# A hybrid attention layer's late phase: another order of the last products, an earlier copy out of PSUM, and one set of loads moved to GpSimd

## The chip, the cores and the metric

The kernel runs as one program on one core of a Trainium2 chip. The metric is the device time of one execution in microseconds (us); smaller is better. Times named "span" run from the first to the last instruction that the profile shows.

## The reference, cut to what matters

```python
def reference(x, w_in, w_out, t5_bias, na_rpb, ln_gain, ln_bias):    # x: (1, 512, 2048), all fp32
    h = einsum('bsd,de->bse', x, w_in[0])                            # 2048 -> 8192 columns
    qa, ka, va, ga, qb, kb, vb, gb = split(h)                        # eight blocks of 1024 columns
    ya = dilated_attention(qa, ka, va, t5_bias)                      # group A: 16 heads of 64
    yb = neighbourhood_attention(qb, kb, vb, na_rpb)                 # group B: 16 heads of 64
    y = concatenate([merge(ya) * silu(ga), merge(yb) * silu(gb)])    # (512, 2048)
    out = einsum('bse,ed->bsd', y, w_out[0])                         # 2048 -> 2048
    return layer_norm(2 ** 0.25 * x + out, ln_gain, ln_bias)
```

## The kernel before

Products of fp32 numbers are made from three float32r matmuls each: every operand is split into a high part (a copy by ScalarE, tiles `wh`, `yk`, `th`) and a low part (a subtraction by VectorE, tiles `wl`, `tl`), and TensorE adds high x high, low x high and high x low. A weight tile of 128x1024 so costs one ScalarE copy and one VectorE subtraction before TensorE may read it.

The work has three stages. First the projections of q, k, v and a part of the gates, in seven products of half size (Strassen's scheme) per block. Then 128 steps of attention: heads go in pairs, 16 pairs of 8 steps each; in each step TensorE makes scores (`scores`), VectorE and ScalarE the softmax, TensorE transposes the probabilities of two steps earlier (`turn`), and every fourth step multiplies them with v (`values`). Between these, `fill` feeds TensorE matmuls of the remaining gates and of the output projection's first columns. Last comes the late phase: the rest of the output projection, the residual and the layer norm.

Names in the attention stage. `turn` transposes into a PSUM bank `pt`, of which there are two; ScalarE copies it to `th`, VectorE subtracts into `tl`, and then the bank is free. Once a pair, in its step 2, `share` transposes the reciprocals of the softmax sums (`den`) into a `pt` bank as well; ScalarE copies that bank to a small row (`tmp<-pt`, 8x128), GpSimd writes it to DRAM (`rc_d`) and later reads it back, spread over the partitions, as `rc`. In the kernel before, copy and write stand in `send`, which runs at the end of the step (`later(0, ...)`, `close`), behind what was put there earlier. `gated` divides an older pair's output by `rc` (VectorE), copies it to the high part `yk` (ScalarE) and writes it to `y_d` in DRAM (GpSimd).

Names in the late phase. The four column groups of the output (512 columns each, numbered 0 to 3) are tiles z[t][dc] for the row blocks t = 0 to 3. Groups 0 and 1 are made in Strassen's seven products (`product`, numbered 1 to 7), groups 2 and 3 directly; the second half of group 3 is "the last column group" (`third` for t = 0, 1, and a loop at the end for t = 2, 3). `jobs` is the list of TensorE work, about 2.7 us each, and `at(n, ...)` hangs work of the other engines on job n; `project` runs them in source order. `convert` splits a weight two jobs ahead, `fetch` loads it through SyncE. `again` reads a pair's y back from `y_d` into one of two buffers (`ysum`), `combine_y`, `high_y` and `low_y` make the sums that Strassen's products need; `starts` lists the jobs of the eight `combine_y`. Work of `put`, `onto`, `done` and `stats` adds the products into z and takes the statistics for the layer norm. `norm` is the layer norm of a row block: VectorE centres, ScalarE scales by 1/sigma, and the bias is added by an accumulating DMA from GpSimd (`z<-in_lbias`); then SyncE stores. `last_norm`, for t = 3, adds the bias on VectorE instead; its bias rows come from matmuls.

What sets the order: each engine takes its instructions in order, and each queue (SyncE's and GpSimd's DMA issues among them) as well. Within the loops the order is the source's (`manual_schedule` for all engines). Behind the loops, for t = 2 and 3, only VectorE is held to the source's order in the kernel before; the other engines' order was set by a scheduler.

Of the kernel before, what the change touches and what calls it, by code (L numbers as in the profile page):

```python
# [6 lines left out]
F32 = mybir.dt.float32  # L7
# [59 lines left out]
AWAKE = 9  # L67
# [4 lines left out]
def hybrid_layer(tc, xT, xn, w_in, w_early, w_mid, w_gate, w_out, t5x, brow, rpb, cmask, eye, gain, lbias, out):  # L72
    nc = tc.nc
    from contextlib import ExitStack
    with ExitStack() as ctx:
# [482 lines left out]
        def later(k, fn, dve=False):  # L558


            tasks.setdefault(step[0] + k, []).append((fn, dve))
# [192 lines left out]
        def share(i):  # L754

            turn8 = bank(pst, "pt")[0:8, 0:128]
            nc.tensor.transpose(turn8, dens[i], ident)

            def send():
                nc.scalar.activation(row, turn8, AF.Copy)  # L760
                nc.gpsimd.dma_start(rc_d[i], row)
                later(1, spread)

            def spread():
                while held and i > 0 and i - 1 not in divided:
                    behind_min(1)
                rc = rc_ring.next("rc")
                for a in range(2):
                    nc.gpsimd.dma_start(rc[64 * a:64 * a + 64], _view(rc_d, 1024 * i + 512 * a, [[0, 64], [1, 512]]))
                rcs[i] = rc  # L770

            later(0, send)
# [103 lines left out]
        late_tiles += [t_d[m][u] for m in (2, 0, 1) for u in range(4)]  # L876
        late_tiles += [w_out[m] for m in (*range(12, 16), *range(28, 32))] + [t_d[3][u] for u in range(4)]
# [95 lines left out]
        c01r, c23r = Ring("n8", "n9"), Ring("n10", "n11")  # L973
        c1_tags = ("n0", "n1", "n2", "n3", "n4", "n6", "n5", "n7")

        def again(i):
            cut_y[i] = yr.next("ysum")[:, :1024].rearrange("p (n q) -> p n q", n=4)
            nc.sync.dma_start(cut_y[i].rearrange("p n q -> p (n q)"), y_d[i].rearrange("p n q -> p (n q)"))
# [58 lines left out]
        def last_weight(u):  # L1037
            wts[u + 4] = [slot(f"r{2 * u + m}", F32R, "wlast") for m in range(2)]
            split(W[28 + u], *wts[u + 4])
# [12 lines left out]
        def norm(t):  # L1052
# [8 lines left out]
            def rescale(i):  # L1061
                zt = z[t][i]
                if t == 2 and i == 3:
                    nc.vector.scalar_tensor_tensor(zt, zt, rs, bb[0], op0=ALU.mult, op1=ALU.add)
                else:
                    nc.scalar.activation(zt, zt, AF.Copy, scale=rs)
                    nc.gpsimd.dma_start(zt, _view(lbias, 512 * i, [[0, 128], [1, 512]]), accum_op=ALU.add)
                nc.sync.dma_start(out[t * 128:t * 128 + 128, 512 * i:512 * i + 512], zt)
# [6 lines left out]
            for i in (0, 2, 3):  # L1075
                centre(i)
                rescale(i)

        accs3 = {}
# [35 lines left out]
        for t in range(4):  # L1115
            at((21, 22, 23, 25)[t], lambda t=t: done(2, t, o2[t]))
        at(34, lambda: done(3, 0, accs3[0]), lambda: norm(0))
        at(36, lambda: done(3, 1, accs3[1]), lambda: norm(1))
        for i in (2, 1):
            at(33 - i, lambda i=i: nc.vector.tensor_tensor(z[3][i], z[3][i], gb[i], ALU.mult))  # L1120
# [5 lines left out]
        with tc.manual_schedule(engines=engines):  # L1126
# [6 lines left out]
            for n in range(132):  # L1133
# [50 lines left out]
                if n in (129, 131):  # L1184
                    project((n - 133) // 2)
# [4 lines left out]
        def shift_rows():  # L1190

            raw, parts = slot("u0", F32, "lnraw"), slot("s0", F32R, "lnparts")
            for i, src in enumerate((gain, lbias)):
                nc.sync.dma_start(raw[:, 12 * i:12 * i + 12].rearrange("p (c j) -> p c j", c=3),
                                  _view(src, 0, [[4, 128], [512, 3], [1, 4]]))
            split(raw[:, :24], parts[:, :24], parts[:, 24:48])
            groups = slot("s1", F32R, "lnrows")
            groups = [groups[:, 512 * i:512 * i + 512] for i in range(3)]
            for r, at in enumerate((0, 24, 0, 12, 36)):
                for c in range(3):  # L1200
                    nc.sync.dma_start(f(groups[c][r:r + 1]), f(parts[:, at + 4 * c:at + 4 * c + 4]))
            return groups

        def last_norm(rows):
# [6 lines left out]
            nc.scalar.activation(rs, mv[:, 1:2], AF.Sqrt, bias=eps)  # L1211

# [4 lines left out]
            queues = [nc.sync, nc.scalar]  # L1217
# [29 lines left out]
        rows = shift_rows()  # L1247
        nms = small.tile([128, 8], F32R, name="nms", bufs=1)
        nc.gpsimd.memset(f(nms), 1.0)
        for t in (2, 3):  # L1250
            acc = bank(pacc, "acc")
            cuts = (slice(0, 256), slice(256, 512)) if t == 3 else (slice(0, 512),)
            accs = [acc] if len(cuts) == 1 else [acc, bank(pss, "sc")]
            for o, part in zip(accs, cuts):
                for u in range(4, 8):
                    list(out_mms(o, t, u, *wts[u], u == 4, u == 7, part))
            if t == 3:
                idle = bank(pss, "sc")
                for _ in range(AWAKE):
                    nc.tensor.matmul(idle, yk[8][:, 0, 0, 0:128], wts[4][0][:, 0:512], start=True, stop=True)  # L1260
            with tc.manual_schedule(engines={mybir.EngineType.DVE}):
                if t == 2:
                    home("t7", 0, 2, 3)
                    for m in range(2):
                        put(0, m + 2, p1[m])
                        stats(0, m + 2)
                    nc.vector.tensor_tensor(z[3][0], z[3][0], gb[0], ALU.mult)
                for m, part in enumerate(cuts):
                    finish(3, t, accs[m], part, 3 + m)
                if t < 3:  # L1270
                    norm(t)
                else:
                    last_norm(rows)
# [65 lines left out]
```

## Time and profile before

| | us |
|---|---|
| median of 3 runs (985.71 to 987.35) | 986.62 |
| the profiled execution | 986.07 |
| its span | 984.3 |
| TensorE busy | 959.6 |
| VectorE busy | 797.3 |
| ScalarE busy | 525.0 |
| GpSimd busy | 219.7 |

The attention stage lies at about 580 to 841 us of the span, the late phase behind it. The profile models the end of a matmul, and matmuls overlap by that model (one of 512 columns is shown as 0.39 us long while the next starts 0.23 us later); so a stall of TensorE is longer than the idle time shown, by the overlap that did not happen.

### The profile page before, as it was taken

What the parts mean: (1) busy time and instruction counts of PE and PEld (TensorE: products, weight loads), DVE (VectorE), ACT (ScalarE), POOL (GpSimd) and SP (SyncE); (2) the same over time, 40 slices, a digit from 0 to 9 for tenths busy, and PEclk for the clock granted to TensorE, in tenths of its full rate; (3) what the DMA queues carried; (4) which work ended last, traced back from release to release, by engine and by line L of the source; (5) the groups of instructions that cost most, each with busy time, mean ns of one, the idle gap of its engine ahead of it and who ended that gap; (6) DMA issues with size and microseconds to landing.
All of it is one profiled execution on the core that took longest, in us unless ns stands there. A gap on an engine that the chain in (4) does not pass through costs nothing.

```text
span 984.3 us, 14233 instructions
## 1 busy us (share of the span) xinstructions
PE 959.6 (97%) x4741; PEld 794.4 (81%) x4741; DVE 797.3 (81%) x1219; ACT 525.0 (53%) x900; POOL 219.7 (22%) x410
## 2 busy tenths in 40 slices
PE   9999999999999999999999999999999999999994
PEld 7878888888888889988888888887878777687883
DVE  8897787779689798897899757888778787789775
ACT  7454443444444444444454457777777777654531
POOL 1006656635741101111111001111111101100021
PEclk9999999999999999999999999999999999999997
DMA  9725796797595296744984887787877877676766
GB/s 339 268 83 124 251 308 205 197 287 212 146 375 189 106 346 202 257 160 147 318 259 143 273 265 252 233 261 241 276 240 269 301 244 233 214 252 226 261 115 175
DMA packets 131273, 227.75 MB, mean 231 GB/s; under 512 B 51247, under 2 KB 71599, under 8 KB 131200
## 3 DMA queue, kind: packets, MB, share of 16 engines
q1 hardware_dynamic: 110544, 179.39, 55.8%
q0 software_dynamic: 20080, 46.81, 16.1%
q8 instruction: 37, 0.61, 0.3%
q10 hardware_dynamic: 576, 0.66, 0.2%
q14 instruction: 36, 0.29, 0.1%
HBM read 169.66 MB, written 57.08 MB: 230 GB/s over the span
## 4 chain that ended last, share of the span: by engine, by line
PE 86%; DVE 5%; ACT 4%; DMA 2%; issue 2%; POOL 0%; DVEq 0%; SPq 0%; ACTq 0%; POOLq 0%
PE acc L405 16%; PE acc L407 16%; PE acc L406 15%; PE acc L601 8%; PE acc L811 5%; PE acc L928 4%; PE pt L726 4%; PE pv L748 4%; PE sc L707 2%; PE sc L706 2%; PE acc L281 2%; PE acc L282 2%; PE acc L283 1%; PE pt L262 1%; PE acc L398 1%
## 5 line engine op out<-in xcount | busy, mean ns | idle before, releaser
L378 ACT ACTIVATE wh<-braw 128x1024 fp32r<-128x1024 f32 x182 | 193.2, 1062 | 268.5 <-PE acc L406 201.0
L383 DVE TENSOR_TENSOR wl<-braw,wh 128x1024 fp32r<-128x1024 f32 x182 | 222.0, 1222 | 41.3 <-ACT wh L378 41.2
L405 PE MATMUL acc<-wh,xk 128*128 128x512 f32 x384 | 151.3, 394 | 0.0
L407 PE MATMUL acc<-wl,xk 128*128 128x512 f32 x384 | 149.7, 390 | 0.0
L406 PE MATMUL acc<-wh,xk 128*128 128x512 f32 x384 | 149.5, 389 | 0.0
L374 DVE TENSOR_TENSOR braw<-braw 128x1024 f32<-128x1024 f32 x104 | 128.4, 1235 | 0.1
L405 PE MATMUL acc<-wh,op 128*128 128x512 f32 x288 | 113.1, 393 | 0.0
L407 PE MATMUL acc<-wl,op 128*128 128x512 f32 x288 | 112.2, 390 | 0.0
L406 PE MATMUL acc<-wh,op 128*128 128x512 f32 x288 | 112.1, 389 | 0.0
L732 DVE TENSOR_TENSOR tl<-pt,th 128x256 fp32r<-128x256 f32 (+1 forms) x128 | 71.1, 556 | 31.6 <-ACT th L731 29.7
L407 PEld LDWEIGHTS acc<-wl,xk 128*128 128x128 f32 x384 | 72.1, 188 | 15.3
L405 PEld LDWEIGHTS acc<-wh,xk 128*128 128x128 f32 x384 | 72.1, 188 | 15.2 <-ACT bias L153 0.9
L406 PEld LDWEIGHTS acc<-wh,xk 128*128 128x128 f32 x384 | 72.2, 188 | 14.5
L601 PE MATMUL acc<-xk,wh 128*128 128x512 f32 x256 | 80.9, 407 | 0.0
L731 ACT ACTIVATE th<-pt 128x256 fp32r<-128x256 f32 (+1 forms) x128 | 62.4, 488 | 31.2 <-PE pt L726 29.3
L663 DVE CUSTOM_DVE_ANT_0 s<-sc,biases 128x512 f32<-128x512 f32 (+2 forms) x128 | 67.7, 529 | 9.6 <-PE sc L707 8.9
L667 ACT ACTIVATE p<-s,mn 128x512 f32<-128x512 f32 (+1 forms) x96 | 62.3, 649 | 24.5 <-DVE mn L663 24.0
L811 PE MATMUL acc<-wh,yk 128*128 128x512 f32 x192 | 67.7, 404 | 0.0
L163 POOL DMA_DIRECT2D bias<-rows_d x128 | 61.3, 487 | 15.2 <-DMA bias<-rows_d 6.2
L407 PEld LDWEIGHTS acc<-wl,op 128*128 128x128 f32 x288 | 54.1, 188 | 11.4
L406 PEld LDWEIGHTS acc<-wh,op 128*128 128x128 f32 x288 | 54.1, 188 | 11.0
L405 PEld LDWEIGHTS acc<-wh,op 128*128 128x128 f32 x288 | 54.1, 188 | 10.8
(202 smaller groups left out, 1864.5 us busy)
## 6 DMA issues: line engine op xcount, KB each, us to landing
braw<-in_w_in SPq DMA_DIRECT2D x96, 512.0 KB
k_d<-kst SPq DMA_DIRECT2D x64, 128.0 KB
q_d<-kst SPq DMA_DIRECT2D x64, 128.0 KB
v_d<-vst SPq DMA_DIRECT2D x32, 256.0 KB
wsum<-in_w_out POOLq DMA_DIRECT2D x32, 256.0 KB, 4.6
t_d<-wsum POOLq DMA_DIRECT2D x32, 256.0 KB, 3.0
q<-q_d SPq DMA_DIRECT2D x32, 256.0 KB
wraw<-in_w_gate SPq DMA_DIRECT2D x16, 512.0 KB
```

Source lines behind the costliest of these rows:

```text
L374: nc.vector.tensor_tensor(raws[q][u], raws[q][u], raws[other][u], ALU.add)
L378: nc.scalar.activation(h, raws[q][u], AF.Copy)
L383: nc.vector.tensor_tensor(l, raws[q][u], f(h), ALU.subtract)
L405: nc.tensor.matmul(accs[t], ah[:, q], h[:, c], start=first and k == 0, stop=False, skip_group_check=skip)
L406: nc.tensor.matmul(accs[t], al[:, q], h[:, c], start=False, stop=False, skip_group_check=skip)
L407: nc.tensor.matmul(accs[t], ah[:, q], l[:, c], start=False, stop=k == 7, skip_group_check=skip)
L601: nc.tensor.matmul(acc, w[:, k * 128:k * 128 + 128], X[8 * u + k][:, s], start=u == 0 and n == 0 and k == 0, stop=u == 1 and n == 2 and k ...
L663: nc.vector.tensor_tensor_reduce(*flat, bias, 1.0, 3e38, ALU.add, ALU.min, mn)
L667: nc.scalar.activation(p[:, to:to + n].rearrange("p (b r c) -> p b r c", r=8, c=c), s[:, :n].rearrange(order, r=8, c=c), AF.Exp, bias=mn, ...
L731: nc.scalar.activation(th, pt[:, :nch], AF.Copy)
L732: nc.vector.tensor_tensor(tl, pt[:, :nch], f(th), ALU.subtract)
L811: nc.tensor.matmul(acc[:, part], yk[k][:, t // 2, s, c], w[:, wk], start=first and kk == 0 and n == 0, stop=last and kk == 1 and n == 2)
```

## The change

It has four parts.

- Attention: `send` is gone. ScalarE's copy of the reciprocals' bank and GpSimd's write of it stand in `share` at once.
- Late phase, order of work: product 4 comes directly after product 3, and `third` for t = 0, 1 behind it (before: `third` first, product 4 last). Product 5 and product 3 exchange PSUM pools. The last pair's division (`gated`) is hung on job 5 and not 3; the `combine_y` are up to one job earlier; `put`, `done`, `onto` and `stats` of groups 0 and 2 are spread over other jobs; the last weights are split at jobs 31 to 34 and not 29 to 32; the first two weights are split two steps earlier in the attention stage.
- The end: for t = 2 and 3 every engine is held to source order. The layer norm of t = 1 stands in the time of t = 2's matmuls and that of t = 2 in the time of t = 3's; t = 2's stores, and its last scaling, wait in a list (`last`) until t = 3's statistics are complete. The last stores alternate from ScalarE's queue on.
- `again` issues its loads of y from GpSimd, not from SyncE.

```diff
@@ share
-            def send():
-                nc.scalar.activation(row, turn8, AF.Copy)
-                nc.gpsimd.dma_start(rc_d[i], row)
-                later(1, spread)
...
-            later(0, send)
+            nc.scalar.activation(row, turn8, AF.Copy)
+            nc.gpsimd.dma_start(rc_d[i], row)
+            later(1, spread)
@@ project, again
-                if n == 3:
+                if n == 5:
                     gated(2 * PAIRS - 1)
...
-            nc.sync.dma_start(cut_y[i].rearrange("p n q -> p (n q)"), y_d[i].rearrange("p n q -> p (n q)"))
+            nc.gpsimd.dma_start(cut_y[i].rearrange("p n q -> p (n q)"), y_d[i].rearrange("p n q -> p (n q)"))
@@ norm
                 if t == 2 and i == 3:
-                    nc.vector.scalar_tensor_tensor(zt, zt, rs, bb[0], op0=ALU.mult, op1=ALU.add)
+                    last.append(lambda: nc.vector.scalar_tensor_tensor(zt, zt, rs, bb[0], op0=ALU.mult, op1=ALU.add))
...
-                nc.sync.dma_start(out[t * 128:t * 128 + 128, 512 * i:512 * i + 512], zt)
+                last.append(lambda: nc.sync.dma_start(out[t * 128:t * 128 + 128, 512 * i:512 * i + 512], zt))
...
+            while last and t < 2:
+                last.pop(0)()
@@ order of the jobs
-        p5 = product(5, pst, 16)
+        p5 = product(5, pacc, 16)
         product(7, None, 20, p1)
-        p3 = product(3, pacc, 24)
+        p3 = product(3, pst, 24)
+        product(4, None, 28, p1)
         for t in range(2):
             jobs.extend(((None, None, lambda w, t=t: third(t)), (None, None, lambda w: None)))
         for u in range(4):
-            at(29 + u, lambda u=u: last_weight(u))
-        product(4, None, 32, p1)
-        starts = (4, 6, 7, 9, 11, 12, 14, 15)
+            at(31 + u, lambda u=u: last_weight(u))
+        starts = (4, 6, 7, 9, 10, 12, 13, 14)
...
-            at(15, lambda t=t: late_x(0, t), lambda t=t: late_x(1, t))
-            at(17 + t, lambda t=t: put(0, t, parts["r1"][t]), lambda t=t: done(0, t, p2[t]))
+            at(18, lambda t=t: late_x(0, t), lambda t=t: late_x(1, t))
+            at(17 + t, lambda t=t: onto(2, t, o2[t]))
+            at(20 + t, lambda t=t: stats(2, t), lambda t=t: put(0, t, parts["r1"][t]))
+            at(21 + t, lambda t=t: done(0, t, p2[t]))
...
-        at(34, lambda: done(3, 0, accs3[0]), lambda: norm(0))
-        at(36, lambda: done(3, 1, accs3[1]), lambda: norm(1))
+        at(38, lambda: done(3, 0, accs3[0]), lambda: norm(0))
@@ attention loop
-                if n in (129, 131):
-                    project((n - 133) // 2)
+                if n in (127, 129):
+                    project((n - 131) // 2)
@@ the end
+            for fn in last:
+                fn()
...
-            queues = [nc.sync, nc.scalar]
+            queues = [nc.scalar, nc.sync]
...
-            with tc.manual_schedule(engines={mybir.EngineType.DVE}):
...
+        with tc.manual_schedule(engines=engines):
...
+                if t == 2:
+                    done(3, 1, accs3[1])
+                    norm(1)
```

Three places show what moved. First ScalarE, step 2 of a pair near the end of the attention stage; `tmp<-pt` is the copy of the reciprocals' bank and `yk<-y` the high part of an older pair's y. Before:

```order
L1152 ACTIVATE tmp<-pv 64x512
L731 ACTIVATE th<-pt 128x256
L790 ACTIVATE yk<-y 128x2x256
L760 ACTIVATE tmp<-pt 8x128
L731 ACTIVATE th<-pt 128x256
```

ScalarE in the same step now:

```order
L1179 ACTIVATE tmp<-pv 64x512
L731 ACTIVATE th<-pt 128x256
L766 ACTIVATE tmp<-pt 8x128
L786 ACTIVATE yk<-y 128x2x256
L731 ACTIVATE th<-pt 128x256
```

The copy of the bank moved ahead of `yk<-y`, directly behind the first `th<-pt`. In 12 of the 15 pairs before, the first `turn` behind `share` is given the reciprocals' bank and waits for that copy; in the other three it is given the bank of the `turn` ahead and waits for VectorE's `tl`. In all 15 pairs now it is given the reciprocals' bank.

Second the loads of y, before in SyncE's queue, among the loads of weights (`lraw`), from the end of the attention stage on:

```order
L884 DMA lraw<-in_w_out 128x1024 x6
L978 DMA ysum<-y_d 128x1024 x2
L884 DMA lraw<-in_w_out 128x1024 x2
L884 DMA lraw<-t_d 128x1024 x3
L978 DMA ysum<-y_d 128x1024
L884 DMA lraw<-t_d 128x1024 x2
L978 DMA ysum<-y_d 128x1024 x2
```

They stand now in GpSimd's queue, from the last pair's reciprocals to the bias's accumulation for t = 0:

```order
L767 DMA rc_d<-tmp 8x128
L787 DMA y_d<-y 128x512
L763 DMA rc<-rc_d 64x512 x2
L974 DMA ysum<-y_d 128x1024 x3
L787 DMA y_d<-y 128x512
L974 DMA ysum<-y_d 128x1024 x5
L1063 DMA z<-in_lbias 128x512 x2
```

All eight loads left SyncE's queue; in GpSimd's the first three stand behind the last pair's `rc` loads, and the other five behind the last write of y.

Third VectorE at the end, from t = 2's last product on (z_7237 is t = 2's column group 3 and z_7238 that of t = 3; `acc` and `sc` are the products' banks). Before:

```order
L1049 TENSOR_TENSOR z_7237<-acc,z_7237 128x512
L1049 TENSOR_TENSOR z_7238<-sc,z_7238 128x256
L1050 BN_STATS st_5088<-z_7237 128x6
L1050 BN_STATS st_5089<-z_7238 128x6
L1070 BN_AGGR mv<-st_5088 128x2
L1210 BN_AGGR mv<-st_5089 128x2
L1059 SCALAR_TENSOR_TENSOR z<-z,mv,gain 128x512
L1073 RECIPROCAL rs<-rs 128x1
L1059 SCALAR_TENSOR_TENSOR z<-z,mv,gain 128x512
L1059 SCALAR_TENSOR_TENSOR z_7237<-z_7237,mv,gain 128x512 x2
L1227 RECIPROCAL rs<-rs 128x1
```

VectorE in the same place now:

```order
L1066 BN_AGGR mv<-st_5088 128x2
L1055 SCALAR_TENSOR_TENSOR z<-z,mv,gain 128x512
L1069 RECIPROCAL rs<-rs 128x1
L1055 SCALAR_TENSOR_TENSOR z<-z,mv,gain 128x512
L1055 SCALAR_TENSOR_TENSOR z_7237<-z_7237,mv,gain 128x512 x2
L1045 TENSOR_TENSOR z_7238<-acc,z_7238 128x256
L1046 BN_STATS st_5089<-z_7238 128x6
L1045 TENSOR_TENSOR z_7238<-sc,z_7238 128x256
L1046 BN_STATS st_5089<-z_7238 128x6
L1223 BN_AGGR mv<-st_5089 128x2
L1060 SCALAR_TENSOR_TENSOR z_7237<-z_7237,rs,gain 128x512
L1242 RECIPROCAL rs<-rs 128x1
```

The whole of t = 2's centring moved ahead of t = 3's last sums; one scaling of t = 2 (L1060) is left between t = 3's statistics and its reciprocal.

More of the change, by code (lines that the diff above doesn't have):

```diff
@@ L1077, in norm, with load_shift, split_shift, spread_shift @@
                 rescale(i)
-        accs3 = {}
+            while last and t < 2:
+                last.pop(0)()
+        def load_shift():
+            raw = slot("u0", F32, "lnraw")
+            for i, src in enumerate((gain, lbias)):
+                nc.sync.dma_start(raw[:, 12 * i:12 * i + 12].rearrange("p (c j) -> p c j", c=3),
+                                  _view(src, 0, [[4, 128], [512, 3], [1, 4]]))
+            rows.append(raw)
+        def split_shift():
+            parts = slot("s0", F32R, "lnparts")
+            split(rows.pop()[:, :24], parts[:, :24], parts[:, 24:48])
+            rows.append(parts)
+        def spread_shift():
+            parts = rows.pop()
+            groups = slot("s1", F32R, "lnrows")
+            rows.extend(groups[:, 512 * i:512 * i + 512] for i in range(3))
+            for r, at_ in enumerate((0, 24, 0, 12, 36)):
+                for c in range(3):
+                    nc.sync.dma_start(f(rows[c][r:r + 1]), f(parts[:, at_ + 4 * c:at_ + 4 * c + 4]))
+        accs3, last = {}, []
         p1 = product(1, pss, 0)
@@ L1245, in last_norm @@
                 rescale(1, part, shifts[2][:, part])
[L1247 to L1260, printed above, removed]
-            with tc.manual_schedule(engines={mybir.EngineType.DVE}):
-                if t == 2:
[L1263 to L1267, printed above, removed]
+        with tc.manual_schedule(engines=engines):
+            nms = small.tile([128, 8], F32R, name="nms", bufs=1)
+            nc.gpsimd.memset(f(nms), 1.0)
+            for t in (2, 3):
+                acc = bank(pacc, "acc")
+                cuts = (slice(0, 256), slice(256, 512)) if t == 3 else (slice(0, 512),)
+                accs = [acc] if len(cuts) == 1 else [acc, bank(pss, "sc")]
+                for o, part in zip(accs, cuts):
+                    for u in range(4, 8):
+                        list(out_mms(o, t, u, *wts[u], u == 4, u == 7, part))
+                if t == 2:
+                    done(3, 1, accs3[1])
+                    norm(1)
+                else:
+                    idle = bank(pss, "sc")
+                    for _ in range(AWAKE):
+                        nc.tensor.matmul(idle, yk[8][:, 0, 0, 0:128], wts[4][0][:, 0:512], start=True, stop=True)
                 for m, part in enumerate(cuts):
                     finish(3, t, accs[m], part, 3 + m)
-                if t < 3:
+                if t == 2:
                     norm(t)
```

35 lines of the change are left out of this document (15 added, 20 removed).

## The prediction

> **What bounds the kernel now.** I read the page's first and fourth parts, then TensorE's waits in the attention stage and in the late phase, then the timeline around each wait, and last the end.
>
> ```profile
> PE 959.6 (97%) x4741; PEld 794.4 (81%) x4741; DVE 797.3 (81%) x1219; ACT 525.0 (53%) x900; POOL 219.7 (22%) x410
> PE 86%; DVE 5%; ACT 4%; DMA 2%; issue 2%; POOL 0%; DVEq 0%; SPq 0%; ACTq 0%; POOLq 0%
> 934.11 10.88 PE acc L811 x48
> ```
>
> TensorE is the bound: 97% busy, 86% of the chain. The third row is a stretch of that chain without stalls: 48 matmuls of 512 columns start one every 10.88/48 = 0.227 us. So a job of 12 matmuls lasts 2.72, one `third` (24) 5.44. The change leaves the matmuls as they are; it can only win back stalls of TensorE and alter the tail behind its last matmul. The stalls that it can reach are in two answers of the waits view (total us, times, longest), first 590 to 841 us, then 841 to 968:
>
> ```profile
> PE pt L726 <- ACT tmp L760: 4.5, 9, 0.5
> PE pt L726 <- DVE tl L732: 1.9, 3, 0.7
> PE acc L928 <- DVE wl L907: 2.9, 6, 0.8
> ```
>
> **Attention: the reciprocals' bank copied at once.** Two kinds of pair, from the timeline (start, duration, engine; the bracket is the idle time and what ended it):
>
> ```profile
> 830.05 0.40 PE L811 MATMUL acc<-wl,yk 128*128 128x512 f32 x1
> 830.95 0.44 PE L726 MATMUL pt<-ident,p 128*128 128x128 f32 x2 [0.50 <-ACT tmp L760]
> 829.85 0.38 ACT L731 ACTIVATE th<-pt 128x256 fp32r<-128x256 f32 x1
> 830.13 0.62 ACT L790 ACTIVATE yk<-y 128x512 fp32r<-128x512 f32 x1
> 830.65 0.25 ACT L760 ACTIVATE tmp<-pt 8x128 f32<-8x128 f32 x1
> 645.41 0.60 ACT L731 ACTIVATE th<-pt 128x512 fp32r<-128x512 f32 x1
> 645.90 1.05 ACT L578 ACTIVATE wh<-wraw 128x1024 fp32r<-128x1024 f32 x1
> 646.14 0.69 DVE L732 TENSOR_TENSOR tl<-pt,th 128x512 fp32r<-128x512 f32 x1
> 646.89 0.66 PE L726 MATMUL pt<-ident,p 128*128 128x128 f32 x4 [0.65 <-DVE tl L732]
> ```
>
> In the first kind TensorE's next `turn` waits for `tmp`, which stands behind the `yk` copy on ScalarE. With `tmp` directly behind `th` it starts at 830.13 instead of 830.65: 0.52 earlier, so the matmul comes at 830.43. The waits view counts 9 such pairs: 9 x 0.52 = 4.7. In the second kind the `turn` waits for `tl`; now it takes the reciprocals' bank, freed by a `tmp` that runs 645.90 to 646.15, so TensorE goes on about 0.05 later, at 646.20 instead of 646.89: 3 x 0.69 = 2.1. The other three of the 15 pairs have `tmp` behind `th` already and give nothing. What ScalarE had in front (`yk`, `wh`) starts 0.25 later; nobody in these rows waits for it within that time. Sum -6.8. What is late next is the following `turn`, which needs the other bank, so `tl`, and the probabilities; if it takes over half of each stall, only 3.4 is left. That is the other end. I take the whole, since a step's other matmuls lie between two turns.
>
> GpSimd's write of the row is issued earlier as well; it waits for `tmp` only, and what stands behind it on GpSimd is idle time.
>
> **Start of the late phase.** The first two weights are split two steps earlier.
>
> ```profile
> 840.22 1.05 ACT L902 ACTIVATE wh<-wraw 128x1024 fp32r<-128x1024 f32 x1
> 841.31 1.22 DVE L907 TENSOR_TENSOR wl<-wraw,wh 128x1024 fp32r<-128x1024 f32 x1 [0.52 <-ACT wh L902]
> 842.59 0.50 PE L928 MATMUL acc<-wl,yk 128*128 128x512 f32 x1 [0.53 <-DVE wl L907]
> 846.22 0.50 PE L928 MATMUL acc<-wl,yk 128*128 128x512 f32 x1 [0.17 <-DVE wl L907]
> ```
>
> Both `wl` waits (0.53 and 0.17) should go, but the copy (1.05) and the subtraction (1.22) now stand ahead of the last `th` and `tl`, for which the last `turn` and `values` wait. I take 0, with 1.2, one subtraction, to either side.
>
> **Late phase: the order of the jobs.** The other four `wl` waits:
>
> ```profile
> 861.25 0.50 PE L928 MATMUL acc<-wl,yk 128*128 128x512 f32 x1 [0.84 <-DVE wl L907]
> 897.20 0.50 PE L928 MATMUL acc<-wl,c 128*128 128x512 f32 x1 [0.29 <-DVE wl L907]
> 900.91 0.50 PE L928 MATMUL acc<-wl,c 128*128 128x512 f32 x1 [0.69 <-DVE wl L907]
> 931.55 0.50 PE L928 MATMUL acc<-wl,c 128*128 128x512 f32 x1 [0.42 <-DVE wl L907]
> 862.00:902.00 40.00, 39.02 (x171) 31.63 (x171) 36.52 (x63) 19.94 (x32) 0.00 (x0) 1.00 0.72 237
> ```
>
> Together 2.24 of idle time shown. A matmul is drawn 0.39 to 0.40 long and follows after 0.23, so each stall is 0.17 longer than shown, and the first matmul behind it takes 0.50, 0.11 more: 2.24 + 4 x 0.28 = 3.3. The last row is the windows view: in these 40 us VectorE (the third busy time) works 36.5, so what is hung on which job decides whether a `wl` is ready. The change takes the last pair's division, the late residuals and several sums out of the jobs ahead of these four, and I let all four waits go. Against it stand the y loads, now GpSimd's:
>
> ```profile
> 861.65 0.37 SPq L978 DMA_DIRECT2D ysum<-y_d  x1
> 867.96 0.69 DVE L983 TENSOR_TENSOR csum<-ysum 128x512 f32<-128x512 f32 x1 [1.57 <-DMA ysum<-y_d]
> 869.49 0.42 DVE L1000 SCALAR_TENSOR_TENSOR yk<-csum,yk 128x256 fp32r<-128x256 f32 x1
> 874.80 0.32 SPq L978 DMA_DIRECT2D ysum<-y_d  x1
> 879.24 0.69 DVE L983 TENSOR_TENSOR csum<-ysum 128x512 f32<-128x512 f32 x1 [0.53 <-DMA ysum<-y_d]
> L769 POOL DMA_DIRECT2D rc<-rc_d x32: 516/532/586, 600.6 to 847.7; - x32
> DMA to landing us min/median/max: 2.6/5.5/7.6
> ```
>
> From SyncE a load takes 6.31 (861.65 to 867.96) or 4.44 (874.80 to 879.24) until VectorE reads it. GpSimd's reads of `rc` (the last two rows) land after 2.6, 5.5 and 7.6. I take L = 6.3, the row for the same tile, with 4.4 and 7.6 as ends. There are two buffers; the odd combines hang on jobs 6, 9, 12 and 14, so from the second to the last are 8 jobs, 21.8 us, for 3 loads and 3 combines of 1.53 (867.96 to 869.49): 3L + 4.6 = 23.5. The 1.7 too much holds up VectorE, and a `wl` stands behind it; as weights are split two jobs ahead, half is covered, and I take 0.8. At 4.4 it is 0. Each further us of L costs 3. That the loads leave SyncE's queue brings weights earlier, but no row of the waits shows TensorE or VectorE waiting for a weight there: 0. The pools of products 3 and 5 are exchanged at the same count of banks: 0. Late phase: -3.3 + 0.8 = -2.5.
>
> The Trainium skill, page "SBUF — State Buffer", section "SBUF: two separate sides", says that GpSimd cannot write descriptors while certain operations of VectorE hold a shared port. By that each y load in this busy stretch would wait, and the slower rival below would come nearer. The 32 `rc` issues of the row above took 516 to 586 ns each beside a busy VectorE, which shows no lockout.
>
> **The tail.** The end hangs on the accumulating DMAs of GpSimd (the first two rows: their count, issue times and latency) and on the stores behind them.
>
> ```profile
> L1067 POOL DMA_DIRECT2D z<-in_lbias x11: 845/867/1359, 944.4 to 972.0; - x11
> DMA to landing us min/median/max: 4.3/6.0/7.4
> 942.15 0.26 DVE L1070 BATCH_NORM_AGGREGATE mv<-st 128x2 f32<-128x24 f32 x1
> 944.41 2.70 POOL L1067 DMA_DIRECT2D z<-in_lbias  x3 [87.93 <-ACT z L1066]
> 949.76 0.86 POOL L1067 DMA_DIRECT2D z<-in_lbias  x1 [2.64 <-issue]
> 958.21 0.85 POOL L1067 DMA_DIRECT2D z<-in_lbias  x1 [1.68 <-issue]
> 967.14 0.42 DVE L1049 TENSOR_TENSOR z<-sc,z 128x256 f32<-128x256 f32 x1 [0.34 <-PE sc L811]
> 971.40 0.15 DVE L1227 RECIPROCAL rs<-rs 128x1 f32<-128x1 f32 x1
> 978.75 0.52 SPq L1068 DMA_DIRECT2D out<-z  x1
> ```
>
> Three go out at 944.41; the fourth only at 949.76, though its input was ready: 5.35 later, about the 6.0 after which the first has landed. The eighth goes at 958.21: (958.21 - 949.76)/4 = 2.11 each. I read that as three in flight at most, 6.0/3 = 2.0.
>
> Call E the time at which VectorE gets the last product, 967.14 here. `third` for t = 0 now ends three `third`s ahead, E - 16.3. Two passes of VectorE and the aggregate (about 1.6), then 2.26 (942.15 to 944.41), put the first accumulation at E - 12.4. All eleven now follow each other closely: the fourth at E - 12.4 + 5.35 = E - 7.05, the eleventh seven later, E - 7.05 + 7 x 2.11 = E + 7.7, landed 6.0 later, at E + 13.7. Before, the last was landed by the store at 978.75, E + 11.6: +2.1. Three stores of that group instead of the one at 978.75 stand last in SyncE's queue, which adds some 0.4: +2.5. VectorE itself wins: its reciprocal, at E + 4.26 now (971.40), comes behind one scaling of t = 2 and not behind its whole centring, some 3.3 earlier. I hide that behind the queue. The ends: all of it shows, and the stores as well, -5; or the queue is slower, 4.3 to 7.4 a piece in threes, +4.
>
> The Trainium skill, page "DMA: Bandwidth & Descriptors", section "Anatomy of one DMA — SWDGE (gpsimd) path", gives 2.0 us plus bytes/436 GB/s: an estimate of 2.6 for these 256 KB. By that three in flight would leave every 0.9 and the queue would not bind, which is the first rival. The row's 6.0 disagrees, and it is this kernel's.
>
> **Sum.** Span 984.3 - 6.8 + 0 - 2.5 + 2.5 = 977.5. The profiled execution is 986.07, 1.77 more than its span, and 0.55 below the median of 986.62. So 977.5 + 1.77 + 0.55 = 979.8 us as the median.
>
> **The rivals.**
>
> - *The accumulations do not bind.* For it: the gaps at 949.76 and 958.21 are marked "issue", a cause that I infer. Against: 2.64 of idle time with input at hand. Then the tail ends with the last row block's own work: -5 instead of +2.5, 972.3.
> - *The next turn takes over.* For it: `tl` is already waited for in three pairs. Against: in the other pairs it wasn't. Half of 6.8 is lost: 983.2.
> - *Slower: late y.* The y loads, in GpSimd's queue behind the last pair's `rc` (which lands after up to 7.6), hold VectorE in front of a `wl` in jobs 8 to 16. At 3 us for each us of L, the forecast's gain of 6.8 is gone at L = 6.3 + 6.8/3 = 8.6; at 9.5 the time is 979.8 + 9.6 = 989.4. For it: a largest landing of 7.6, in a stretch where DMA is 72% busy (the windows row). Against: the median of 5.5.
> - *No measurable change.* Attention wins nothing, since `turn` waits for the probabilities at once, and the tail takes the rest: 986.6.
>
> **How the numbers follow.** Forecast 0.57, first rival 0.15, second 0.17, late y 0.07, no change 0.04. A measurement of this kernel tells about 0.2%, 2 us, from no change. Faster: the first three, 0.89, and what of late y falls short of 8.6, 0.9 in all; within 0.2% 0.05; slower 0.05. The range runs from 972, just past the first rival, to 984.5, past the second and past attention at half with a y load of 6.8; what is left out are late y, no change and sums of several low ends.
>
> **What the profile would show.** Attention: the waits of the `turn` for `tmp` at 0.25 or less each, those for `tl` at that place gone; wrong if the same waits reappear under `tl` or `p`. Late phase: no `wl` wait over 0.3 in the jobs from 16 on; one or two new ones behind a combine that waits for `ysum`. Loads: landing medians of `ysum` between 4.4 and 7.6; beyond 8.6 the forecast falls. Tail: eleven accumulations issued 2.1 apart from the fourth on, the last store more than 17.2 us (984.3 - 967.14) behind the start of VectorE on the last product, by about 2.5; wrong if VectorE's last scaling and its own store end last.

## The result, and the profile after

| | before | after |
|---|---|---|
| median, us | 986.16 (985.54 to 987.35, 4 runs) | 980.29 (979.43 to 981.69, 4 runs) |
| ratio, 95% interval | | 0.994 (0.9923 to 0.9958) |
| span of the profiled execution, us | 984.3 | 979.9 |

The forecast was 979.8. Beside other kernels on another occasion the changed kernel gave 980.17 against 985.69, 0.9944 (0.9930 to 0.9958). The profiled execution of 979.9 was the longest of the four; the others had 977.6 to 978.8.

The page's first and fourth parts for the changed kernel:

```profile
PE 957.9 (98%) x4741; PEld 794.4 (81%) x4741; DVE 797.3 (81%) x1219; ACT 526.1 (54%) x900; POOL 234.6 (24%) x418
PE 86%; issue 6%; DMA 3%; DVE 2%; ACT 1%; POOL 1%; POOLq 0%; SPq 0%; DVEq 0%; ACTq 0%
```

TensorE does the same 4741 matmuls in 1.7 us less. In the chain "issue" (time in which an engine waited for nothing that the profile shows) rose from 2% to 6%; its last four steps are now issues, the first and the last of them these, GpSimd between two accumulating DMAs:

```profile
957.29 2.18 issue
...
966.55 1.60 issue
```

To see where the time went I cut both executions at three starts that the timeline shows: the first scores of the attention stage, the first matmul of product 1, and VectorE's last sum (`z<-sc,z`, the E of the prediction). Before (its third row, 967.14, stands in the prediction):

```profile
574.84 0.39 PE L706 MATMUL sc<-k,q 128*128 128x512 f32 x1
841.35 0.71 PE L928 MATMUL acc<-wh,yk 128*128 128x512 f32 x2
```

After:

```profile
576.31 0.39 PE L706 MATMUL sc<-k,q 128*128 128x512 f32 x1
837.66 0.70 PE L924 MATMUL acc<-wh,yk 128*128 128x512 f32 x2
961.33 0.42 DVE L1045 TENSOR_TENSOR z<-sc,z 128x256 f32<-128x256 f32 x1 [0.40 <-PE sc L807]
```

The lengths that follow, with those of the experiments cut at the same three starts:

| kernel | attention | late phase | tail | span |
|---|---|---|---|---|
| before | 266.51 | 125.79 | 17.16 | 984.3 |
| after | 261.35 | 123.67 | 18.57 | 979.9 |
| after, second profile | 261.28 | 122.39 | 19.68 | 978.4 |
| copy at once alone | 260.38 | 123.77 | 17.23 | 977.7 |
| copy at once in the last pair alone | 266.55 | 125.15 | 17.25 | 985.7 |
| copy at once, first weights earlier | 261.37 | 123.10 | 17.25 | 978.1 |
| copy at once, y loads on GpSimd | 260.43 | 122.63 | 17.43 | 976.2 |
| after, y loads on SyncE | 261.33 | 122.29 | 19.80 | 978.8 |
| after, nine accumulations | 261.37 | 123.13 | 16.59 | 976.7 |
| after, no accumulations | 261.28 | 121.82 | 9.46 | 967.6 |
| copy at once, new end, old order | 260.41 | 127.25 | 12.39 | 976.4 |
| the same in one source order | 260.46 | 126.87 | 11.76 | 974.4 |
| the same, y loads on GpSimd | 260.38 | 124.38 | 12.48 | 973.1 |
| the same, job 38, stores on ScalarE's queue | 260.38 | 122.59 | 12.54 | 970.5 |

So the attention stage gave 5.2, the late phase 2.1 and 3.4 in the two profiles, and the tail took 1.4 and 2.5 back. What lies ahead of the first scores (574.84 and 576.31) isn't touched by the change and differs by 1.5 between the two executions; the second profile began at 575.04.

**Attention.** TensorE's waits from 590 to 841 us, after:

```profile
PE pv L748 <- DVE tl L732: 0.7, 1, 0.7
PE pv L748 <- DVE mn L663: 0.5, 1, 0.5
PE acc L924 <- DVE y L1180: 0.3, 1, 0.3
PE sc L706 <- DVE mn L663: 0.2, 1, 0.2
PE pv L748 <- ACT th L731: 0.2, 1, 0.2
```

Both groups of `turn` waits (4.5 and 1.9) are gone. The step that the prediction showed at 829.85 to 830.95 now reads:

```profile
825.74 0.38 ACT L731 ACTIVATE th<-pt 128x256 fp32r<-128x256 f32 x1
826.02 0.25 ACT L766 ACTIVATE tmp<-pt 8x128 f32<-8x128 f32 x1
826.18 0.61 ACT L786 ACTIVATE yk<-y 128x512 fp32r<-128x512 f32 x1
826.33 0.44 PE L726 MATMUL pt<-ident,p 128*128 128x128 f32 x2
```

From `th` to the `turn` it was 1.10 and is 0.59.

**Late phase.** VectorE's first wait for a y load, and the waits of TensorE for a `wl`:

```profile
852.57 0.69 DVE L979 TENSOR_TENSOR csum<-ysum 128x512 f32<-128x512 f32 x1 [3.71 <-DMA ysum<-y_d]
855.97 0.50 PE L924 MATMUL acc<-wl,yk 128*128 128x512 f32 x1 [0.62 <-DVE wl L903]
862.36 0.50 PE L807 MATMUL acc<-wl,yk 128*128 128x512 f32 x1 [0.62 <-DVE wl L903]
936.66 0.50 PE L924 MATMUL acc<-wl,yk 128*128 128x512 f32 x1 [0.54 <-DVE wl L903]
```

The waits at 897.20 and 900.91 are gone, and the two of the first weights (842.59, 846.22) as well. In their place are one in product 2 and one at the first weight of group 2's second half, both behind VectorE's wait of 3.71, and one at product 4's last weight. In the second profile of the same kernel only one of the early two is left:

```profile
859.74 0.50 PE L807 MATMUL acc<-wl,yk 128*128 128x512 f32 x1 [0.30 <-DVE wl L903]
```

The landing times of the eight y loads in the first profile:

```profile
DMA to landing us min/median/max: 3.4/4.6/9.8
```

The two longest, 7.9 and 9.8, are the first two, which stand right behind the last reciprocals; the other six are below the 6.3 that I took.

**Tail.** ScalarE's scaling of t = 0, GpSimd's accumulations, their landing times, VectorE's last scalings and SyncE's stores:

```profile
947.31 2.70 ACT L1062 ACTIVATE z<-z,rs 128x512 f32<-128x512 f32 x4 [0.56 <-DVE rs L1069]
948.46 2.71 POOL L1063 DMA_DIRECT2D z<-in_lbias  x3 [71.78 <-ACT z L1062]
953.27 0.85 POOL L1063 DMA_DIRECT2D z<-in_lbias  x1 [2.10 <-issue]
968.18 0.87 POOL L1063 DMA_DIRECT2D z<-in_lbias  x1 [1.62 <-issue]
DMA to landing us min/median/max: 4.5/6.1/6.4
965.21 2.19 DVE L1236 SCALAR_TENSOR_TENSOR z<-z,rs,acc 128x512 f32<-128x512 f32 x4
962.80 12.39 SPq L1064 DMA_DIRECT2D out<-z  x7
975.28 1.19 SPq L1239 DMA_DIRECT2D out<-z  x2
```

VectorE is through at 967.40. The eleventh accumulation is only issued at 968.18 and lands some 6.2 later; t = 2's stores stand behind it in SyncE's queue (7 stores, 12.39), and the last two of t = 3 behind those. The end, 979.9, comes 12.5 after VectorE's.

The windows view shows what the core's sixteen DMA engines did meanwhile. The last two numbers of a row are their mean busy share, which can come out a little over 1, and GB/s:

```profile
950.00:953.00 3.00, 3.00 (x15) 2.50 (x14) 2.76 (x6) 0.56 (x3) 1.17 (x2) 1.00 0.84 124
953.00:975.00 22.00, 11.59 (x73) 9.77 (x71) 12.76 (x27) 5.35 (x10) 6.89 (x8) 0.85 1.04 256
975.00:978.00 3.00, 0.00 (x0) 0.00 (x0) 0.00 (x0) 0.00 (x0) 0.00 (x0) 0.50 0.98 353
```

The first three accumulations alone take 0.84 of these engines and move 124 GB/s; the last stores alone move 353. From 953 to 975, with both, the engines are full. So two accounts fit the 2.1 us from one accumulation to the next: a queue that lets no more than three out, which the prediction has, and DMA engines that get through no more. The experiments change the number of accumulations, and with it both; none tells the two apart.

### The profile page after: what moved, and what is told of

Its sections match the earlier page's. It is cut to its first block, busy times and chain, and to the rows that moved or that the text cites. A ratio compares the mean times of both kernels' runs of the same rounds, so it can differ in the third digit from the quotient of the medians.

```text
span 979.9 us, 14247 instructions
## 1 busy us (share of the span) xinstructions
PE 957.9 (98%) x4741; PEld 794.4 (81%) x4741; DVE 797.3 (81%) x1219; ACT 526.1 (54%) x900; POOL 234.6 (24%) x418
## 4 chain that ended last, share of the span: by engine, by line
PE 86%; issue 6%; DMA 3%; DVE 2%; ACT 1%; POOL 1%; POOLq 0%; SPq 0%; DVEq 0%; ACTq 0%
PE acc L405 16%; PE acc L407 16%; PE acc L406 16%; PE acc L601 9%; PE acc L924 5%; PE acc L807 5%; PE pt L726 3%; PE pv L748 3%; DMA rc_d<-tmp 2%; PE sc L707 2%; PE sc L706 2%; PE pt L262 1%; PE acc L281 1%; PE acc L283 1%; PE acc L282 1%
```

## The experiments

Each ratio is to the kernel before, run beside it.

### The copy at once alone

```diff
 (kernel before)
-            later(0, send)
+            nc.scalar.activation(row, turn8, AF.Copy)
+            nc.gpsimd.dma_start(rc_d[i], row)
+            later(1, spread)
```

> The kernel before with the attention edit alone: ScalarE's copy of the reciprocals' bank and GpSimd's write of it stand in share at once; jobs, y loads and tail as before. Theory (the first turn no longer waits behind yk, 12 pairs at 0.5 to 0.7, two of them taken up by a new wait): 986.2 - 6.1 = 980.1 us, within 0.7. Rival (the next turn takes up half, the gain seen came from the late phase): 983.2. Rival (the attention edit is worth nothing alone): 986.2.

Measured: 979.0 against 986.83, ratio 0.9921 (0.9909 to 0.9934). The edit of these lines gives the whole gain of the change, by the medians somewhat more (the changed kernel has 0.9940 and 0.9944; the intervals overlap). The attention stage is 6.13 shorter. At the `turn` each of the twelve pairs for which a gain was forecast saves 0.52 to 0.69; in one of them (the step at 778.36 before) 0.6 of it is lost again within that step. The late phase is 2.0 shorter as well in this profile, though nothing in it was moved. TensorE's waits from 833 to 960 us show where these 2.0 lie:

```profile
PE acc L924 <- DVE wl L903: 1.4, 4, 0.5
```

Before it was 2.9 in six waits. With 0.28 for each of the two stalls less, as the prediction counts them, that is 2.1.

The changed kernel once more, on another occasion:

> The changed kernel once more, beside the others on the same chip: 980.3 by its first four runs, 0.9940 of the kernel before. If the kernel with the copy at once alone (979.0, 0.9921) is really faster than it, this comes out again at 980 to 981.

It came out again at 980.17, 0.9944; whether the edit alone is faster than the whole isn't settled by these intervals.

### The last pair alone

```diff
-            later(0, send)
+            send() if i == 15 else later(0, send)
```

> The kernel before with the copy at once in the last pair's share alone; the other 15 pairs, jobs, loads and tail as before. The kernel with the copy at once in all pairs gained 7.8, of which its trace shows 6.1 ahead of the late phase and 2.0 in it. Theory (the 2.0 come from the last pair's reciprocals, which are written 1.5 sooner behind the end of the attention stage, so that the last division and the weights behind it on VectorE are sooner): 986.8 - 2.0 = 984.8. Rival (the 2.0 are another thing, such as transfers falling otherwise): 986.8.

Measured: 985.54 against 985.69, 0.9996 (0.9987 to 1.0006), late phase 125.15. That theory falls: the last pair's reciprocals don't explain the 2.0. What brings VectorE's `wl` forward there stays open. The late phase of one and the same program differs by 1.3 between two profiles (123.67 and 122.39), so a part of it may be how transfers fall.

### The first weights earlier

```diff
 (copy at once alone)
-                if n in (129, 131):
-                    project((n - 133) // 2)
+                if n in (127, 129):
+                    project((n - 131) // 2)
```

> The kernel before with the copy at once and the first two weights split two steps earlier. Theory (the first weights' split stands ahead of the last th and tl and costs the last values 0.93, and saves two waits of the first job of 0.81 and 0.29 with their restarts): attention stage 261.3 instead of 260.4, the late phase shorter by about 1.2, in all 0.3 less. Rival (the 0.93 belongs to another part of the change): the attention stage stays at 260.4.

Measured, one run: 979.9. The attention stage is 261.37, 0.99 longer than without; the late phase is 0.67 shorter. TensorE's waits from 833 to 842 us show the exchange:

```profile
PE pv L748 <- DVE tl L732: 0.7, 1, 0.7
PE acc L924 <- DVE y L1149: 0.3, 1, 0.3
```

The last values wait for a `tl` that stands behind a `wl`, and in place of the first `wl` a product waits for y. By these two profiles the edit costs 0.3 in sum, which they can't tell from nothing.

### The y loads: SyncE or GpSimd

```diff
 (first: changed kernel with)               (second: copy at once alone with)
-                nc.gpsimd.dma_start(cut_y  |  -                nc.sync.dma_start(cut_y
+                nc.sync.dma_start(cut_y    |  +                nc.gpsimd.dma_start(cut_y
```

> The changed kernel with the eight y loads back in SyncE's queue. Theory (the first y load, behind the last reciprocals in GpSimd's queue, lands late, VectorE waits 3.7 for it ahead of a wl, and two stalls of TensorE of 0.90 and 0.89 hang on that): both go, 980.3 - 1.8 = 978.5. Rival (the stalls come from VectorE's order and not from the loads): 980.3. Rival (the loads hold up weights in SyncE's queue): 981 to 983.

> The kernel before with the copy at once and, besides, the y loads issued by GpSimd; order of the late products and tail as before. Theory (in GpSimd's queue the first y loads wait behind the last reciprocals and hold VectorE, which costs TensorE 0.9 to 1.8): 979.9 to 980.8. Rival (the loads cost nothing, the changed kernel's two stalls come from its order): 979.0. Rival (the loads are better off there, as weights come sooner through SyncE): 978.

Measured: 980.57, 0.9934 (0.9921 to 0.9946), for the changed kernel with SyncE's loads; 978.59, 0.9929 (0.9917 to 0.9942), for the old order with GpSimd's. Neither moves the time. In the first the two early stalls are gone from the trace and the late phase is 122.29, but the tail is 19.80: the accumulations decide the end, not VectorE. The price of the loads, on either queue, is below what these runs can tell.

### Fewer accumulations, and none

```diff
 (changed kernel, nine)                     (changed kernel, none)
-                if t == 2 and i == 3:      |  -  nc.gpsimd.dma_start(zt, ..., accum_op=ALU.add)
-                    last.append(lambda: ...)
+                if i == 3:
+                    last.append(add_bias)
```

> The changed kernel with the bias of column group 3 added by VectorE for all row blocks (before only for t = 2): nine accumulating DMAs instead of eleven. Theory (the end hangs on accumulations of which three are in flight, 2.1 us each): 980.3 - 4.2 = 976.1. Rival (the end hangs on the last row block's own work or on the stores): 980.3, within 1.

> The changed kernel with all eleven accumulating DMAs left out, so the bias of those tiles is not added. Theory (they alone set the end): VectorE's last scaling ended at 967.40 in the profile, the last store comes 0.3 later and takes 4.0 as there (975.86 to 979.9): 971.7 of span instead of 979.9, so 980.3 - 8.2 = 972.1. Rival (the stores themselves queue): 976. Rival (not binding): 980.3.

Measured: 978.21, 0.9913 (0.9898 to 0.9927), with nine; 970.88, 0.9837 (0.9820 to 0.9855), with none. Without them the tail is 9.46, and E to VectorE's end is the same 6.0: the accumulations, and the stores that wait for them, hold the end by 9 to 10 us. The DMA engines, full behind E in the changed kernel, have a mean share of 0.44 from E on here. With nine I had forecast 4.2 less and got 2.0 to 2.1 by the medians, 2.7 to 3.1 by the ratios. GpSimd's rows show one reason:

```profile
947.25 2.70 POOL L1066 DMA_DIRECT2D z<-in_lbias  x3 [71.84 <-ACT z L1065]
952.68 0.85 POOL L1066 DMA_DIRECT2D z<-in_lbias  x1 [2.72 <-ACT z L1065]
959.67 0.86 POOL L1066 DMA_DIRECT2D z<-in_lbias  x1 [3.25 <-ACT z L1065]
963.87 0.86 POOL L1066 DMA_DIRECT2D z<-in_lbias  x1 [1.17 <-ACT lnleft L1253]
```

With three tiles to a row block the fourth accumulation belongs to t = 1 and waits for its scaling until 952.68: the queue isn't filled ahead. The last goes at 963.87 instead of 968.18, 4.3 earlier on the clock of the trace but 3.1 earlier against E (960.11 here), and by the trace it took 7.2 to land, 1.0 more than the changed kernel's. The other account fits as well: by the DMA view the accumulations took 42.0% of the sixteen engines' time from 940 to 980 us with eleven and 36.3% with nine, which is 2.3 us less.

### The new end with the old order of the products

The kernel before with the copy at once and the whole of the changed kernel's end (`last`, source order on every engine, t = 2's layer norm ahead of t = 3's sums), but `third` for t = 0 and 1 ahead of product 4, as before.

```diff
 (changed kernel, and the tables of jobs as before)
-        product(4, None, 28, p1)
         for t in range(2):
             jobs.extend(((None, None, lambda w, t=t: third(t)), (None, None, lambda w: None)))
+        product(4, None, 32, p1)
...
                 if t == 2:
-                    done(3, 1, accs3[1])
-                    norm(1)
+                    home("t7", 0, 2, 3)
+                    for m in range(2):
+                        put(0, m + 2, p1[m])
+                        stats(0, m + 2)
+                    nc.vector.tensor_tensor(z[3][0], z[3][0], gb[0], ALU.mult)
```

> The kernel before with the copy at once and the changed kernel's end (t = 2's layer norm ahead of t = 3's last sums, every engine in source order), but the old order of the late products (third for t = 0 and 1 ahead of product 4) and the y loads in SyncE's queue. Theory (the changed kernel's end is short in itself, and its gain is eaten since eleven accumulations, three in flight, all come within 16 us of the last product; with product 4 in between eight of them are through by then): the tail is VectorE's 6.1 behind the last product plus 3.6 for the last store, 9.7 instead of 17.2, so 979.0 - 7.5 = 971.5, up to 973 if t = 2's accumulations hold the last stores. Rival (the new end itself gives nothing): 979. Rival (the end is bound by the stores): 976.

Measured: 978.96, 0.9932 (0.9920 to 0.9945): 7.5 worse than expected. VectorE, in the timeline:

```profile
955.38 0.69 DVE L814 SCALAR_TENSOR_TENSOR z<-xl,acc 128x512 f32<-128x512 f32 x1 [6.30 <-PE acc L924]
964.01 0.41 DVE L1045 TENSOR_TENSOR z<-sc,z 128x256 f32<-128x256 f32 x1
```

TensorE still ran 28 and then 13 matmuls of the last two row blocks between those of product 4: product 4 stands in the loops' block of source order and the last row blocks in a block of their own, and between two blocks the scheduler mixes. So VectorE waited 6.30 for product 4, and its centring of t = 2, now ahead of t = 3's sums, came into the way of these: its last sum starts 3.6 after the last product ends.

```profile
957.31 3.04 PE L807 MATMUL sc<-wlast,yk 128*128 128x256 f32 x24
```

The tail behind that sum fell from 17.2 to 12.4 (976.4 - 964.01), so the end is short by itself; the wait ahead of it took most of that.

### One source order for all of it

The same, with the end in the loops' own block and the layer norms of t = 0 and 1 on jobs 35 and 37 instead of 34 and 36; then with the y loads on GpSimd; then with the layer norm of t = 1 on job 38 and t = 3's stores all on ScalarE's queue:

```diff
             for n in range(len(jobs)):
                 project(n)
-        with tc.manual_schedule(engines=engines):
             nms = small.tile([128, 8], F32R, name="nms", bufs=1)
...
-        at(37, lambda: done(3, 1, accs3[1]), lambda: norm(1))
+        at(38, lambda: done(3, 1, accs3[1]), lambda: norm(1))
...
-            queues = [nc.scalar, nc.sync]
+            queues = [nc.scalar]
```

> The kernel before with the copy at once and the new end, the old order of the late products, y loads in SyncE's queue; but the last two row blocks of the last column group stand in the same source order as the jobs, so that TensorE runs them behind product 4 and not between its matmuls (in the earlier kernel with the new end, t = 2's 24 matmuls and 13 of t = 3's were moved ahead of product 4's end, and VectorE waited for that). The layer norms of t = 0 and 1 hang one job later (35 and 37). Theory (the end is then VectorE's 6.1 behind the last product and some 4.4 for the last store, and eight of eleven accumulations are through): tail 10.5 to 11 instead of 17.2, so 0.9921 of the kernel before less 6.5 us: 972 to 973 (0.986). Rival (VectorE and the accumulations of t = 2 hold the end anyway): tail 12.4 as in the earlier kernel, but TensorE 1.8 sooner: 976 to 977. Rival (new stalls at product 4 take it back): 979.

> The same, with the y loads issued by GpSimd. By the trace of the kernel with the copy at once and the loads on GpSimd the late phase was 1.1 shorter than with SyncE's: 971 to 972. Rival (that difference was chance between two traces of the late phase, which differ by 1.3 for the changed kernel itself): the same as with SyncE's loads, within 0.7.

> The last kernel (copy at once, new end, old order of the late products, one source order, y loads on GpSimd) with two edits: the layer norm of t = 1 hangs on job 38 instead of 37, so no wl of product 4 stands behind it, and all of t = 3's stores go out on ScalarE's queue, so none stands behind t = 2's stores that wait for accumulations. Theory: the stall of 1.76 at product 4 goes, the last store is issued some 0.7 sooner: 975.1 - 2.5 = 972.6 (0.9865). Rival (the accumulations of t = 2, some 6 us after their issue, set the end): only the stall goes, 973.4. Rival (t = 1's accumulations come later and hold those of t = 2): 975.

Measured: 975.70, 0.9894 (0.9877 to 0.9910); 975.08, 0.9890 (0.9875 to 0.9905); 974.32, 0.9882 (0.9865 to 0.9898). All three beat the kernel before and the changed kernel: their intervals lie wholly below the changed kernel's (0.9923 to 0.9958 and 0.9930 to 0.9958). The first was forecast 3 too low: TensorE waited 1.49 for a `wl` of product 4 behind the layer norm of t = 1,

```profile
948.82 0.50 PE L924 MATMUL acc<-wl,yk 128*128 128x512 f32 x1 [1.49 <-DVE wl L903]
```

and its tail was 11.76, not 10.5 to 11. The loads on GpSimd change nothing that can be told (0.6). In the last the stall is gone, the median is 0.8 lower where 2.5 was forecast, and its tail is 12.54. By the timeline it is the accumulations of t = 2 that hold it; they go out with nothing in flight ahead of them:

```profile
950.75 0.86 POOL L1063 DMA_DIRECT2D z<-in_lbias  x1 [2.84 <-issue]
955.94 2.66 POOL L1063 DMA_DIRECT2D z<-in_lbias  x3 [4.22 <-ACT z L1062]
957.96 0.42 DVE L1045 TENSOR_TENSOR z<-sc,z 128x256 f32<-128x256 f32 x1 [0.40 <-PE sc L807]
955.88 9.74 SPq L1064 DMA_DIRECT2D out<-z  x5
```

Eight accumulations are issued by 950.75, the last three from 955.94 on, 2 us ahead of E; the last store of t = 2 is out at 965.6. These three, 5 to 7 us after issue, and their stores are by the timeline what is left of the tail over the 9.46 without accumulations; no run leaves them out of this kernel. The DMA engines are full here too, by the windows view: a share of 1.07 from 958 to 962, at 140 GB/s, and of 1.05 from 962 to 968, at 361.

## Why the prediction was right, and where it wasn't

The sum was 979.8 and the median is 980.29. The three stages gave -5.9 and -6.1 in the two profiles of the changed kernel where the sum has -6.8 + 0 - 2.5 + 2.5 = -6.8. The attention edit and the tail went the way that was worked out; the terms for the late phase and the y loads are right in size, in part for other reasons, and so far by luck.

- **Attention, -6.8.** The copy at once alone shortens the stage by 6.13 (266.51 to 260.38). Each pair gave what its rows said: 0.51 at 829.85, now 825.74. The 0.7 short of 6.8 is for the most part the one pair that lost its gain again; the waits view has two that weren't there, `sc` for `mn` and `pv` for `th`, 0.2 each besides the overlap. So a later wait takes over in one pair of twelve, and the rival that halves the gain falls. The expectations written for the experiments said two pairs; it is one.
- **Start of the late phase, 0 with 1.2 to either side.** +0.99 in the attention stage and -0.67 in the late phase. The bound was right. For the whole change the stage so gives -5.2.
- **Late phase, -2.5.** Two profiles give -2.1 and -3.4, but the working was only half right. It let four waits go; two went (897.20, 900.91), one stayed behind the y loads and one came back at product 4's last weight (0.54, where the prediction would see none over 0.3 from job 16 on). Nor are the two that went shown to be the new order's work: in five of the seven kernels that have the copy at once and the old order they are gone as well. What filled the sum up are the first weights' two waits, booked at 0, and a late phase that came out 2.0 shorter with the copy at once alone, which had no term. Since that can't be told from the difference between two profiles, the late order's own worth is not shown; it is not more than a microsecond or two.
- **y loads, 0.8 of stall.** The first two took longer than the 6.3 that I put in (7.9 and 9.8), and the first held VectorE for 3.71; the later six took less (in the second profile one of them took 7.4). Two stalls of 0.9 with their overlap in one profile, one of 0.6 in the other. The mechanism of the slower rival is there, far from its price, and since the accumulations set the end, moving the loads back changed nothing.
- **Tail, +2.5.** +1.4 and +2.5 in the two profiles, with the issue times as worked out: the first accumulation at E - 12.9 (forecast -12.4), the eleventh at E + 6.9 (forecast + 7.7), and VectorE through at E + 6.1, hidden. What the working left out are the DMA engines, full from 953 on, so that the 2.11 which it took from the rows may be theirs and not the queue's. The rival by which accumulations don't bind falls with the kernel that has none (970.88). With it falls what the rule of the Trainium skill would make of the time, page "DMA: Bandwidth & Descriptors", section "Anatomy of one DMA — SWDGE (gpsimd) path": the estimate of 2.6 us for one such transfer stands against a median of 6.1 here, with three under way, and a least of 4.5.

What the prediction didn't say is the balance inside it: the copy at once alone has 0.9921 (0.9909 to 0.9934) and the whole change 0.9940 and 0.9944 (0.9930 to 0.9958 the second time). The reordering, the loads and the new end together gave nothing that can be told, and by the ratios cost about 2 us, by the medians 1.2 to 1.3 (the intervals overlap). The new end has a tail of 11.8 to 12.5 instead of 17.2 where most accumulations are through in time, some 5 us; the new order of the products takes that away, since it brings `third` to the end and with it all eleven accumulations behind E - 12.9. With the old order, eight are issued 7 us ahead of E, and the same end reaches 974.32.

## What to carry to other kernels

When work is moved toward the end of a program, count what it puts into the slowest queue that the end still waits for: here eleven transfers of 6 us with three in flight held the end by 9 us. The rows of the five compute engines don't show it; the DMA share does, with 1.04 from 953 to 975. A small copy on which the next user of a PSUM bank waits is worth putting directly behind the bank's last write, ahead of what else its engine has ready: here it gave 0.5 to 0.7 a pair. And a part of a change is worth running alone: a few lines of this one made the whole gain, and the rest only paid once the old order of the products was put back.

## What the chip showed

- GpSimd's accumulating DMAs of 256 KB: after three have gone out, each further one is issued as an earlier one lands, by the trace 0.31 us behind it in the changed kernel, with two others still under way each time. There the first goes at 948.46, lands 4.5 later, and the fourth goes at 953.27, 4.8 after the first; its input was ready (ScalarE's scaling of the four tiles ended at 950.01). It was an inference from gaps before; in no profile here are more than three under way.
- The landing times have medians of 6.0 before, 6.1 and 6.7 after, 6.0 in the kernel of 974.32. Of three that go out together the later ones take longer: 4.5, 5.7 and 6.3 for the first three of the changed kernel.
- Three such transfers alone keep the sixteen DMA engines busy for 0.84 of the time while moving 124 GB/s; plain stores of z move 353 GB/s at 0.98 (both in the changed kernel).
- The late phase of one program differs by 1.3 us between two profiles, while the attention stage agrees within 0.1 (261.28 to 261.37 in six profiles with the first weights early, 260.38 to 260.46 in six with the copy at once and them late). A difference of 1 us in the late phase of single profiles proves nothing.
